# Retention's v projection first, on operands without norm and shift; new unit orders in both mixers; half of layer 0's mix through DRAM

## Chip and metric

One core of a Trainium2 chip runs the whole program in one launch. The metric is the device time of an execution in microseconds. A run without profile gives the time alone; one more execution was profiled, and all rows of the trace come from that one.

## What is computed

Two decoder layers over 1024 tokens of width 1024, all in float32. In each, a conditioning vector c gives by one large product six columns (shift, scale, gate for the mixer, the same for the MLP) of 1024 channels.

```
for layer in range(2):
    mod = silu(c) @ ada_w[layer] + ada_b[layer]              # 1024 x 6144
    sh_m, sc_m, gt_m, sh_f, sc_f, gt_f = split(mod, 6)
    h = rmsnorm(x, norm_mix_w[layer]) * (1 + sc_m) + sh_m
    y = even_mixer(h) if layer == 0 else odd_mixer(h)
    x = x + gt_m * y
    h = rmsnorm(x, norm_mlp_w[layer]) * (1 + sc_f) + sh_f
    x = x + gt_f * (square(relu(h @ w1)) @ w2)
return rmsnorm(x, final_norm_w)
```

The even mixer projects h to x, y (a gated linear recurrence, RG-LRU), and q, k, v, g (chunkwise retention with 4 heads of 128, rotary q and k, a norm per head, and a silu gate g). The odd mixer projects to Q, F, I, G (HGRN2) and q, k, v, z (gated DeltaNet). Both concatenate their two parts to `mix` and multiply by an output matrix.

## The kernel before

**Layout.** Activations lie with channels on partitions: x is 8 tiles of 128 channels for each of two halves (f) of 512 tokens. A projection is cut into units of 128 output channels: the 24 units of the even mixer are x0 to x3, y0 to y3 and q, k, v, g of the heads 0 to 3. For full precision every operand is split into a rounded high part (on ScalarE) and a low remainder (by a subtraction on VectorE), `split` (L599). `mm3` (L732) then does three matmuls for each of the 8 channel tiles, high x high, high x low and low x high, each 128x512: 24 dense matmuls for a unit and half, 48 for a unit.

**Order.** Every operation is recorded first (`Recorder`, L158), with an engine, a duration that is assumed, and a priority: its place in the program plus a bias. `place` (L218) then simulates the engines and lets each take, of what is ready and has free buffers, the operation with the lowest number. So the program order steers, and the order found is fixed for each engine. All DMAs go through SP's queue (a few through POOL's). Dense matmuls have the bias BIG, thus lowest priority: any other ready matmul goes ahead. Buffers: 73 tiles of 128x512 in `heap`, 4 of 128x1024 in `raw` (weights as loaded), 6 in `w` (their high and low parts, two for a unit), 3 PSUM banks `dps` for dense results and 5 `psum` for all others; `raw`, `w`, `dps`, `pad` and `blk` are given out in program order.

**Weights.** `push` (L623) loads the next unit into `raw` and splits it; `pop` (L684) keeps three ahead and, while the ninth to the fortieth unit are loaded, adds two ada units for each. An ada unit (`ada_unit`, L759) loads 512 KB of modulation rows into `raw` and multiplies them by csil (silu(c) on all partitions, a `blk` tile) with a running sum on VectorE: one of the 96 columns of `mod`. What is left of the 80 ada units is done in the down projection of layer 0's MLP, one in every third of its 112 steps from step 32 on (L1025). `ada_until(0)`, `ada_bias` and `ada_wsc` (L1440 to L1443) then finish the columns of layer 1, `wsc` being the scale times the norm's weight.

**Start (L1161 to L1218).** x half 0 is loaded, csil is made, and the norm factor of half 0 by squares, a sum over channels on TensorE and two activations (`rstd_half`, L797). Then for each of 8 channel tiles j: the shift column comes from 16 matmul passes with one output column (`ccol`) and a small transpose, the scale column from two multiplies with a running sum (512 wide, `blk`), and `first_operand` (L1180) makes h and splits it. Each j loads 1 MB of modulation rows. The first three weight units are split with the subtraction on POOL, and the norm of half 1 adds its squares on POOL too. Then `first = dense(hh, LEAD, pmt)` (L1407) does x0, x1 and q0 together.

**Mixer of layer 0 (L1406 to L1430).** The loop goes through EVEN_ORDER (L436); "l2" ends the recurrence of the two x units before it (`lru_out`, L1317). A v unit's result is copied out of PSUM, and `ret_item` (L1362) turns it by four transposes and an eviction (`to_token_major`, L1353) into tokens on partitions, which the two products with v need. `split_mix` (L1146) splits `mix` for `out_proj` (L847) and can fetch parts from the DRAM tensor `ms`; layer 0 keeps all of mix in SBUF, layer 1 sends that of its first three heads through `ms`. Layer 1's loop (L1823 to L1850) follows ODD_ORDER (L451) in the same way.

## Time and profile before

| | us |
|---|---|
| median of 3 runs | 2313.14 (2312.41 to 2313.26) |
| profiled execution | 2310.03 |
| its span, first to last instruction | 2308.3 |
| TensorE busy | 2272.8 |
| VectorE busy | 1698.1 |
| ScalarE busy | 1278.1 |
| units of layer 0's mixer, about | 24 to 350 |
| its output projection, about | 350 to 435 |
| MLP of layer 0, about | 435 to 1069 |
| mixer of layer 1 with its output projection, about | 1069 to 1650 |

Nearly all instructions are recorded by one helper, so every line reads L342; groups are told apart by the tiles that they write and read. Matmuls overlap, and their ends are modelled: the step from one start to the next is the pace, not the mean ns of one.

### The profile page before, as it was taken

To read this page: it belongs to the slowest core of one execution; us is meant where nothing else is said; L and a number is where in the kernel's file an instruction comes from. 1 tells how busy PE (TensorE), PEld (TensorE's weight loads), DVE (VectorE), ACT (ScalarE), POOL (GpSimd) and SP (SyncE) were. 2 spreads that over 40 slices of the span, in tenths; PEclk is the share of its full clock that TensorE was granted. 3 is DMA by queue.
4 is the path that set the end of the run, shared out by engine and by line. 5 is a ranking of instruction groups with operands and counts; after the bars stand their busy time and mean duration, and the time that the engine had idled before them with its cause. 6 is when DMAs were issued, how large, how long until landed. Compare 5 with 4: busy or idle time off the path is not lost.

```text
span 2308.3 us, 31439 instructions
## 1 busy us (share of the span) xinstructions
PE 2272.8 (98%) x10906; PEld 1868.4 (81%) x10906; DVE 1698.1 (74%) x2830; ACT 1278.1 (55%) x2377; POOL 330.7 (14%) x474
## 2 busy tenths in 40 slices
PE   7999999999999999999999999999999999999998
PEld 4778888878888888887887888878888888888886
DVE  7998668996665867888876687566687666765776
ACT  5788454575555444455755575646465555544444
POOL 3000000010000101000264335440001000111100
PEclk9999999999999999999999999999999999999999
DMA  8243338867665989643213122153358664997742
GB/s 296 82 135 121 113 119 287 285 188 230 193 183 159 335 299 307 213 147 99 77 44 81 50 61 69 57 153 125 127 170 253 193 192 146 292 301 231 178 133 96
DMA packets 199075, 393.34 MB, mean 170 GB/s; under 512 B 30146, under 2 KB 40962, under 8 KB 198916
## 3 DMA queue, kind: packets, MB, share of 16 engines
q1 hardware_dynamic: 180484, 357.78, 46.1%
q0 software_dynamic: 18432, 33.56, 9.0%
q8 instruction: 85, 1.39, 0.2%
q14 instruction: 74, 0.61, 0.1%
HBM read 308.91 MB, written 82.35 MB: 170 GB/s over the span
## 4 chain that ended last, share of the span: by engine, by line
PE 81%; issue 6%; DVE 5%; ACT 5%; DMA 3%; SPq 0%; POOL 0%; POOLq 0%; DVEq 0%; ACTq 0%
PE psum L342 41%; PE dps L342 40%; ACT heap L342 3%; DVE heap L342 3%; DMA raw<-in_dram 1%; DMA heap<-in_dram 1%; DVE w L342 1%; ACT w L342 1%; DMA heap<-h_spill 1%; DVE raw L342 1%; SPq L342 0%; DMA h_spill<-heap 0%; ACT L342 0%; ACT pad L342 0%; POOL heap L342 0%
## 5 line engine op out<-in xcount | busy, mean ns | idle before, releaser
L342 PE MATMUL dps<-heap,w 128*128 128x512 f32 x5016 | 1241.4, 395 | 7.7 <-DVE heap L342 4.1
L342 PEld LDWEIGHTS dps<-heap,w 128*128 128x128 f32 x5016 | 926.7, 188 | 200.9 <-DVE heap L342 6.4
L342 PE MATMUL psum<-heap,w 128*128 128x512 f32 x3816 | 890.5, 389 | 2.3 <-DVE heap L342 1.8
L342 PEld LDWEIGHTS psum<-heap,w 128*128 128x128 f32 x3816 | 715.7, 188 | 154.3 <-DVE heap L342 3.8
L342 ACT ACTIVATE heap<-heap 128x512 f32<-128x512 f32 (+2 forms) x1055 | 617.0, 609 | 184.3 <-DVE heap L342 162.2
L342 DVE TENSOR_TENSOR heap<-heap,heap 128x512 f32<-128x512 f32 (+1 forms) x863 | 579.7, 695 | 79.0 <-ACT heap L342 72.7
L342 ACT ACTIVATE w<-raw 128x512 fp32r<-128x512 f32 (+1 forms) x248 | 193.3, 782 | 219.5 <-PE dps L342 101.6
L342 ACT ACTIVATE w<-heap 128x512 fp32r<-128x512 f32 x224 | 141.5, 632 | 297.9 <-PE psum L342 274.8
L342 DVE TENSOR_TENSOR w<-raw,w 128x512 fp32r<-128x512 f32 (+1 forms) x213 | 194.3, 915 | 96.4 <-ACT w L342 90.7
L342 DVE TENSOR_TENSOR w<-heap,w 128x512 fp32r<-128x512 f32 x192 | 132.3, 689 | 120.0 <-ACT w L342 119.6
L342 POOL TENSOR_TENSOR blk<-blk,blk 32x31 f32<-32x31 f32 (+15 forms) x248 | 169.8, 685 | 34.2 <-issue 9.6
L342 POOL DMA_DIRECT2D raw<-in_dram x32 | 27.8, 870 | 768.9 <-DMA x_spill<-heap 283.2
L342 ACT ACTIVATE heap<-psum 128x512 f32<-128x512 f32 (+6 forms) x189 | 89.8, 482 | 82.8 <-PE psum L342 81.6
L342 PE MATMUL psum<-heap,heap 128*128 128x128 f32 (+4 forms) x1064 | 128.0, 264 | 2.2 <-DVE heap L342 1.7
L342 PEld LDWEIGHTS psum<-heap,heap 128*128 128x128 f32 (+2 forms) x1064 | 112.6, 169 | 21.6 <-DVE heap L342 3.9
L342 POOL DMA_DIRECT2D heap<-in_dram x64 | 55.7, 870 | 440.0 <-DMA heap<-in_dram 157.6
L342 DVE SCALAR_TENSOR_TENSOR raw<-raw,blk 128x1024 f32<-128x1024 f32 x80 | 97.0, 1218 | 4.7 <-DMA raw<-in_dram 4.7
L342 DVE TENSOR_TENSOR heap<-psum,heap 128x512 f32<-128x512 f32 x89 | 61.1, 687 | 41.6 <-PE psum L342 36.3
L342 ACT ACTIVATE heap<-dps 128x512 f32<-128x512 f32 (+1 forms) x134 | 77.7, 586 | 23.0 <-PE dps L342 14.1
L342 ACT ACTIVATE w<-pad 128x512 fp32r<-128x512 f32 x64 | 40.5, 633 | 88.6 <-PE psum L342 55.6
L342 DVE SCALAR_TENSOR_TENSOR heap<-pad,col,heap 128x512 f32<-128x512 f32 x96 | 78.3, 819 | 0.3
L342 DVE TENSOR_TENSOR w<-pad,w 128x512 fp32r<-128x512 f32 x64 | 44.1, 690 | 39.3 <-ACT w L342 39.2
(180 smaller groups left out, 1270.2 us busy)
## 6 DMA issues: line engine op xcount, KB each, us to landing
raw<-in_dram SPq DMA_DIRECT2D x232, 512.0 KB, 4.3
heap<-in_dram SPq DMA_DIRECT2D x226, 256.0 KB, 5.6
h_spill<-heap SPq DMA_DIRECT2D x224, 256.0 KB, 4.5
heap<-h_spill SPq DMA_DIRECT2D x224, 256.0 KB, 5.3
heap<-in_dram POOLq DMA_DIRECT2D x64, 256.0 KB, 6.7
x_spill<-heap SPq DMA_DIRECT2D x48, 256.0 KB, 2.9
heap<-x_spill SPq DMA_DIRECT2D x48, 256.0 KB, 5.3
pad<-in_dram SPq DMA_DIRECT2D x32, 256.0 KB, 2.8
```

The costliest lines, as they stand in the source:

```text
L342: op.call(*a, **k)
```

## The change

The four v units move to the front and no longer use h. For each j, as soon as its scale column and its x tile are there, `plain_operand` makes x times (1 + scale) times the norm's weight, split in two. `lead_tile` multiplies 128 tokens of it (as the stationary operand) by the 512 columns of all four heads' v weights, 24 dense matmuls for each of 8 token tiles, so that the result has tokens on partitions. The shift columns are computed afterwards, four of them on TensorE and four on VectorE. A ninth `lead_tile` on the shift columns, repeated over 128 tokens, gives `lead_bias`. The norm factor, turned to a column by eight transposes, multiplies the eight tiles, and lead_bias is added. `ret_item` reads these tiles. The squares of the norm wait for the last plain operand, and POOL takes no part. h is made after that, and units are then done one at a time. One ada unit goes with each of the loads 5 to 24, two with 25 to 40, and the rest with every third step of the down projection from step 28 on. Mix of heads 0 and 1 of both kinds goes through `ms`. Both orders of units are new.

```
 EVEN_ORDER = [(w[0], int(w[1])) for w in
-              "x0 x1 l2 q0 k0 v0 x2 x3 l2 q1 k1 v1 y0 y1 q2 k2 v2 y2 q3 k3 v3 y3 g0 g1 g2 g3".split()]
+              "x0 x1 q0 k0 x2 l2 q1 k1 x3 l2 q2 k2 y0 g0 q3 y1 k3 g1 g2 y2 y3 g3".split()]
 ODD_ORDER = [(w[0], int(w[1])) for w in
-             "q0 k0 v0 F0 Q0 I0 q1 k1 v1 G0 F1 Q1 q2 z0 I1 k2 v2 F2 G1 q3 Q2 k3 z1 z2 I2 F3 Q3 v3 G2 I3 G3 z3".split()]
+             "q0 k0 v0 F0 Q0 I0 q1 k1 v1 G0 F1 Q1 q2 k2 I1 z0 v2 F2 G1 q3 Q2 k3 I2 v3 z1 F3 Q3 z2 G2 I3 G3 z3".split()]
 def push():
-            split(hi, lo, raw, (), G if i < LEAD else V)
+            split(hi, lo, raw)
+    def lead_unit():
+        i = state["next"]
+        state["next"] = i + 1
+        raw = rec.tile("raw")
+        dma(raw, units[i])
+        if i < 3:
+            hi, lo = rec.tile("w", F32R), rec.tile("w", F32R)
+            split(hi, lo, raw)
+            lead_w.extend((hi[:, c], lo[:, c]) for c in (slice(0, HT), slice(HT, D)))
+        else:
+            for c in (slice(0, HT), slice(HT, D)):
+                hi, lo = hsplit_tiles()
+                split(hi, lo, raw[:, c])
+                lead_w.append((hi, lo))
 def pop():
-            if 8 < n <= 40:
-                ada_some(2)
+            if 4 < n <= 40:
+                ada_some(1 if n <= 24 else 2)
 def mlp(l, xh):
-            if l == 0 and n >= 32 and n % 3 == 1:
+            if l == 0 and n >= 28 and n % 3 == 1:
                 ada_some(1, [marks[-1]])
...
+    def plain_operand(f, j):
+        w = wsc[:, j:j + 1]
+        hi, lo = hsplit_tiles()
+        act(hi, xh[f][j], AF.Copy, scale=w)
+        plain[f].append((hi, lo))
+        return V.scalar_tensor_tensor(lo, xh[f][j], w, hi.bitcast(F32), ALU.mult, ALU.subtract)
     for j in range(KC):
+        if j % 2 == 0:
+            lead_unit()
+        xh[0].append(ht("x"))
+        dma(xh[0][j], xT[j, :, 0:HT])
+        for q in range(2):
+            a = ht("ada")
+            dma(a, ada[4 + j][:, q * HT:(q + 1) * HT])
+            V.scalar_tensor_tensor(a, a, 1.0, csil[:, q * HT:(q + 1) * HT], ALU.mult, ALU.mult,
+                                   accum_out=acc[:, j, q:q + 1])
...
+        plain_operand(0, j)
+    xh[1] = load_half(xT, 1)
+    for j in range(KC):
+        plain_done = plain_operand(1, j)
+    shift_raw = {}
+    for j in (0, 4, 1, 5, 2, 6, 3, 7):
+        for q in range(2):
+            a = shift_raw[j, q] = ht("ada")
+            dma(a, (ada0[j] if j < 4 else ada[j - 4])[:, q * HT:(q + 1) * HT])
+    rec.bias = 0
+    def lead_tile(ps, his, los):
+        mm3(ps, his, los, range(KC), [w[0] for w in lead_w], [w[1] for w in lead_w])
+        y = ht("y")
+        act(y, ps, AF.Copy)
+        return y
+    for f in range(2):
+        for n in range(4):
+            c = slice(n * P, n * P + P)
+            lead[f].append(lead_tile(pdt() if n < 3 else pmt(), [h[:, c] for h, _ in plain[f]], [l[:, c] for _, l in plain[f]]))
...
+    rs = [rstd_half(xh[f], after=[plain_done]) for f in range(2)]
...
+    lead_bias = lead_tile(pmt(), [a[0] for a in sh], [a[1] for a in sh])
+    pm, rstok = pmt(), small("rstok", [8])
+    for f in range(2):
+        for n in range(4):
+            T.transpose(pm[:, 4 * f + n:4 * f + n + 1], rs[f][0:1, n * P:n * P + P], ident[0:1, 0:1])
+    V.tensor_copy(rstok, pm[:, 0:8])
+    for f in range(2):
+        scaled(f, rs[f])
+        for k in range(KC):
+            hh[f].append(first_operand(f, k))
+    for f in range(2):
+        for n in range(4):
+            V.scalar_tensor_tensor(lead[f][n], lead[f][n], rstok[:, 4 * f + n:4 * f + n + 1], lead_bias, ALU.mult, ALU.add)
 def ret_item(h, f, q, k):
-        vt = to_token_major(vT)
+        vt = [v[:, h * P:h * P + P] for v in vtok[f]]
...
-    first = dense(hh, LEAD, pmt)
     for kind, h in EVEN_ORDER:
-        pss = first.pop(0) if first else dense(hh)
+        pss = dense(hh)
...
+            elif kind in "yg":
+                ch = h + (4 if kind == "g" else 0)
+                (lru_gelu if kind == "y" else gate_mix)(ps, mix[f][ch])
+                if h < 2:
+                    dma(ms[f, ch], mix[f][ch])
+                    mix[f][ch] = None
-    out_proj(split_mix(mix, late), xh, 0)
+    out_proj(split_mix(mix, late, ms), xh, 0)
```

## Rows read from the trace of the kernel before

**Rows 1.** The page, part 1: busy time of each engine, its share of the span, and instructions (x).

```profile
PE 2272.8 (98%) x10906; PEld 1868.4 (81%) x10906; DVE 1698.1 (74%) x2830; ACT 1278.1 (55%) x2377; POOL 330.7 (14%) x474
```

**Rows 2.** The windows view of stretches of the start and of the mixer of layer 0: length, then busy time and instructions (x) of TensorE's matmuls (PE), its weight loads (PEld), VectorE (DVE), ScalarE (ACT) and GpSimd (POOL), the granted clock (1.00 is 2.4 GHz), the DMA share and GB/s.

```profile
0.00:13.00 13.00, 3.89 (x17) 3.58 (x18) 7.13 (x25) 9.07 (x19) 1.34 (x7) 1.00 0.84 282
...
22.00:48.00 26.00, 22.88 (x135) 14.29 (x134) 23.22 (x48) 14.25 (x29) 14.67 (x8) 0.93 0.96 340
...
90.00:150.00 60.00, 58.92 (x295) 48.90 (x294) 58.70 (x114) 44.77 (x83) 1.01 (x1) 1.00 0.41 124
```

**Rows 3.** The windows view again, columns as in rows 2, of the rest of layer 0's mixer, of the mixer of layer 1, of 50 us within it, and of the end of layer 0's MLP.

```profile
90.00:350.00 260.00, 257.62 (x1297) 215.00 (x1296) 206.35 (x396) 173.54 (x393) 3.63 (x4) 1.00 0.40 121
1080.00:1660.00 580.00, 573.37 (x3259) 477.05 (x3259) 413.63 (x701) 348.61 (x696) 196.86 (x326) 0.99 0.27 82
1200.00:1250.00 50.00, 46.48 (x256) 39.18 (x255) 34.22 (x54) 32.09 (x62) 6.43 (x19) 0.93 0.32 87
1054.00:1069.00 15.00, 15.00 (x69) 12.08 (x68) 5.02 (x7) 4.51 (x7) 0.00 (x0) 1.00 0.27 90
```

**Rows 4.** Groups of TensorE's instructions from 0 to 90 us, shapes kept apart: what is written and read, shapes, count (x), busy us and mean ns of one, idle time before them and what ended it.

```profile
L342 PE MATMUL dps<-heap,w 128*128 128x512 f32 x120 | 31.0, 401 | 0.2 <-POOL w L342 0.2
...
L342 PE MATMUL psum<-heap,w 128*128 128x512 f32 x72 | 17.7, 396 | 0.8 <-DVE heap L342 0.6
...
L342 PE MATMUL psum<-heap,ones_f 1*128 1x512 f32 x4 | 2.2, 640 | 0.0
```

**Rows 5.** The timeline of TensorE in the start: start, length of the run of like instructions, what, count (x), idle time before it and what ended it.

```profile
12.86 3.15 PE L342 MATMUL psum<-heap,ccol 128*1 128x128 f32 x14 [3.13 <-DMA heap<-in_dram]
...
22.60 1.91 PE L342 MATMUL psum<-heap,ccol 128*1 128x128 f32 x16
...
32.20 3.53 PE L342 MATMUL psum<-heap,ccol 128*1 128x128 f32 x16 [2.23 <-DMA heap<-in_dram]
...
78.92 11.04 PE L342 MATMUL dps<-heap,w 128*128 128x512 f32 x48
89.80 0.39 PE L342 MATMUL psum<-heap,heap 128*128 128x512 f32 x1
```

**Rows 6.** The rates of all DMA queues from 0 to 60 us, GB/s in 40 slices of 1.5 us.

```profile
GB/s 0 145 305 269 320 361 403 374 410 403 392 382 389 404 388 391 377 389 385 382 384 386 388 388 382 392 392 364 184 57 186 336 388 264 6 11 0 0 0 0
```

**Rows 7.** The timeline of all engines from 9.5 to 19 us, columns as in rows 5.

```profile
9.77 0.60 ACT L342 ACTIVATE blk<-psum 128x512 f32<-128x512 f32 x1 [0.29 <-PE psum L342]
...
13.24 0.63 ACT L342 ACTIVATE heap<-heap 128x512 fp32r<-128x512 f32 x1
13.31 2.34 POOL L342 TENSOR_TENSOR w<-raw,w 128x1024 fp32r<-128x1024 f32 x1 [11.43 <-ACT w L342]
13.90 2.30 DVE L342 TENSOR_TENSOR heap<-heap,heap 128x512 fp32r<-128x512 f32 x1 [0.70 <-ACT heap L342]
...
16.12 0.68 DVE L342 SCALAR_TENSOR_TENSOR heap<-heap,blk 128x512 f32<-128x512 f32 x1
...
16.73 0.68 DVE L342 SCALAR_TENSOR_TENSOR heap<-heap,blk 128x512 f32<-128x512 f32 x1
...
18.23 0.16 DVE L342 SCALAR_TENSOR_TENSOR wsc<-mod,col 128x1 f32<-128x1 f32 x1
```

**Rows 8.** Groups of VectorE's instructions from 0 to 90 us, columns as in rows 4.

```profile
L342 DVE SCALAR_TENSOR_TENSOR heap<-heap,blk 128x512 f32<-128x512 f32 x16 | 16.1, 1011 | 0.0
L342 DVE TENSOR_TENSOR heap<-heap,heap 128x512 fp32r<-128x512 f32 x19 | 14.3, 772 | 4.8 <-ACT heap L342 4.6
...
L342 DVE TENSOR_TENSOR w<-raw,w 128x1024 fp32r<-128x1024 f32 x3 | 3.7, 1223 | 0.3 <-ACT w L342 0.3
L342 DVE SCALAR_TENSOR_TENSOR wsc<-mod,col 128x1 f32<-128x1 f32 x8 | 3.3, 415 | 0.0
```

**Rows 9.** The timeline of TensorE in the mixer of layer 1, columns as in rows 5.

```profile
1213.61 0.60 PE L342 MATMUL psum<-ident,heap 128*128 128x128 f32 x4
1213.96 0.48 PE L342 MATMUL psum<-heap,ones_r 128*128 128x512 f32 x1
1217.97 0.80 PE L342 MATMUL dps<-heap,w 128*128 128x512 f32 x1 [3.52 <-DVE heap L342]
```

**Rows 10.** The view of one tensor, the DRAM tensor that layer 1's mix already goes through: its transfers with the issue times in ns (min, median, max), first and last start, and the time from issue to landing in us.

```profile
L342 SPq DMA_DIRECT2D heap<-mix_spill x12: 320/423/639, 1545.0 to 1552.0; - x12
...
DMA to landing us min/median/max: 2.0/4.3/6.2
```

**Rows 11.** Groups of VectorE's instructions from 90 to 350 us, columns as in rows 4.

```profile
L342 DVE SCALAR_TENSOR_TENSOR raw<-raw,blk 128x1024 f32<-128x1024 f32 x37 | 45.0, 1217 | 3.5 <-DMA raw<-in_dram 3.5
...
L342 DVE SCALAR_TENSOR_TENSOR heap<-pad,col,heap 128x512 f32<-128x512 f32 x19 | 14.0, 743 | 0.0
```

**Rows 12.** The timeline of VectorE around the end of layer 0's MLP, columns as in rows 5.

```profile
982.61 1.22 DVE L342 SCALAR_TENSOR_TENSOR raw<-raw,blk 128x1024 f32<-128x1024 f32 x1
...
993.53 0.24 DVE L342 SCALAR_TENSOR_TENSOR wsc<-mod,col 128x8 f32<-128x8 f32 x2
...
1031.82 1.41 DVE L342 SCALAR_TENSOR_TENSOR heap<-heap,wsc,heap 128x512 f32<-128x512 f32 x2
...
1052.92 0.75 DVE L342 SCALAR_TENSOR_TENSOR heap<-heap,mod,heap 128x512 fp32r<-128x512 f32 x1
```

**Rows 13.** The timeline of TensorE there, columns as in rows 5.

```profile
1058.22 8.33 PE L342 MATMUL dps<-heap,w 128*128 128x512 f32 x36
```

More of the change, by code (lines that the diff above doesn't have):

```diff
@@ L606, in trunk_kernel @@
     units = []
+    lead_w = []
     loads = {}
@@ L760, in ada_unit @@
         a = rec.tile("raw")
-        dma(a, ada[48 * l + j - 8], after)
+        dma(a, ada[48 * l + j - 4], after)
         acc = mod[:, 48 * l + j:48 * l + j + 1]
@@ L794, in column_sum, with rstd_half @@
         T.matmul(ps, ones_x, lo, start=False, stop=True)
-    def rstd_half(xh, eng=V, last=False):
+    def rstd_half(xh, eng=V, last=False, after=()):
         order = (4, 5, 6, 7, 0, 1, 2, 3) if last else range(KC)
         ssum = ht("ssum")
-        act(ssum, xh[order[0]], AF.Square)
+        act(ssum, xh[order[0]], AF.Square, after)
         for k in order[1:]:
             sq = ht("sq")
-            act(sq, xh[k], AF.Square)
+            act(sq, xh[k], AF.Square, after)
             if not last or k != order[-1]:
@@ L1182, in first_operand @@
         act(h, xh[f][k], AF.Identity, scale=wsc[:, k:k + 1], bias=mod[:, k:k + 1])
-        hh[f].append(operand(h))
-    scaled(0, rs0)
+        return operand(h)
     acc = small("ada0", [8, 2])
-    hh = [[], []]
-    for j in range(KC):
-        if j in (0, 1, 3):
-            with bias(2 * BIG):
-                push()
+    plain = [[], []]
+    def plain_operand(f, j):
[4 more added lines that the diff above has]
+        return V.scalar_tensor_tensor(lo, xh[f][j], w, hi.bitcast(F32), ALU.mult, ALU.subtract)
@@ new lines, in trunk_kernel @@
+    for f in range(2):
+        for n in range(4):
+            c = slice(n * P, n * P + P)
+            lead[f].append(lead_tile(pdt() if n < 3 else pmt(), [h[:, c] for h, _ in plain[f]], [l[:, c] for _, l in plain[f]]))
+    for j in range(4, KC):
+        for q in range(2):
+            a = shift_raw[j, q]
+            V.scalar_tensor_tensor(a, a, 1.0, csil[:, q * HT:(q + 1) * HT], ALU.mult, ALU.mult,
+                                   accum_out=acc[:, j, q:q + 1])
+        V.scalar_tensor_tensor(mod[:, j:j + 1], acc[:, j, 0:1], cc("ada_b", j), acc[:, j, 1:2], ALU.add, ALU.add)
@@ L1192, in trunk_kernel @@
+    for j in range(4):
         pm, row = pmt(), rec.tile("s")
         for q in range(2):
-            a = ht("ada")
-            dma(a, ada0[j][:, q * HT:(q + 1) * HT])
+            a = shift_raw[j, q]
             for k in range(4):
@@ L1371, in ret_item @@
         pkv = pmt()
-        for s in sl4:
-            T.matmul(pkv[:, s], kt[:, s], vt[:, s], start=True, stop=True)
+        for n, s in enumerate(sl4):
+            T.matmul(pkv[:, s], kt[:, s], vt[n], start=True, stop=True)
         st = ht("st")
@@ L1383, in ret_item @@
         po = pmt()
-        for s in sl4:
-            T.matmul(po[:, s], sc[:, s], vt[:, s], start=True, stop=before is None)
+        for n, s in enumerate(sl4):
+            T.matmul(po[:, s], sc[:, s], vt[n], start=True, stop=before is None)
             if before is not None:
@@ L1821, in hg_item @@
         act(m, pot, AF.Copy, scale=cc("hnw"))
-    first, got, fg = dense(hh, LEAD), {}, {}
+    first, got, fg = dense(hh, 3), {}, {}
     for kind, h in ODD_ORDER:
```

54 lines of the change are left out of this document (22 added, 32 removed).

## The prediction

> **What bounds it now.** I read the page first: TensorE is busy 98% of the span, VectorE 74% [rows 1]. So time can come from two places only: TensorE work that disappears, and stretches in which TensorE waits or runs slowly. The windows view places the second kind [rows 2]: in the first 13 us TensorE works 3.9, and between 22 and 48 us it works 22.9 of 26 with the granted clock at 0.93 on the mean. After 90 us it loses little: in 260 us to the end of layer 0's mixer it idles 2.4, and 6.6 of 580 us in the mixer of layer 1 [rows 3]. The loss is in the start.
>
> How large is it? The instruction groups of the first 90 us [rows 4] count 120 + 72 = 192 dense 128x512 matmuls, four units of the 24 of layer 0. Warm, 48 of them took from 78.92 to 89.80 us [rows 5], 0.2267 us each, so 192 are worth 43.5 us. They were done at 89.8 us. The other 46 us hold the modulation columns, the norm, and waiting. The timeline [rows 5] shows why: x0, x1 and q0 need the shift, the scale and the norm of all 1024 channels, thus 8 MB of modulation rows, and the DMA engines deliver 380 to 400 GB/s without a gap from 10 to 41 us [rows 6].
>
> **What the change does there.** The four v units come first, on x times its scale column only. The norm factor multiplies the result per token, and the shift comes back as one added row, lead_bias. The sum is made for the moment at which TensorE has done 192 dense matmuls and all preparation, 89.8 us now.
>
> 1. First dense matmul. csil is complete at 9.77 + 0.60 = 10.4 us [rows 7]. Constants, one v unit, one tile of x and one scale row are 1.5 MB, there by 7.5 us by the rates of [rows 6]. After csil: the second accumulating multiply at its pitch of 0.61, two one-column operations of 0.16 and the rounded half on ScalarE, 0.63 [rows 7], with hand-overs: 12.5 us.
> 2. Feeding it. A step of eight needs one x tile, one scale row and half a v unit, 1.05 MB, 2.7 us at 390 GB/s. VectorE pays 2 x 0.61 + 0.4 + 0.65 for the low half, and half of a weight split of 1.22 [rows 8]: 2.9 us. TensorE consumes a step in 12 matmuls, 2.72 us. All three are nearly equal, and TensorE starts on the slow clock, so I charge no wait: the eighth operand is wanted at about 35 us; VectorE has it at 10.4 + 8 x 2.9 = 33.6 and DMA at 26.
> 3. Dense work, 192 x 0.2267: 43.5 us.
> 4. The slow clock. The one-column passes took 3.15 us for 14 from 12.86 and 1.91 for 16 from 22.60 [rows 5]: the clock column has nothing on it, but by this pace TensorE went from 1.2 to 2.4 GHz only at about 22 us, after working from 12.86 on with small gaps. That is 9.5 us at half rate. The fall after an idle 2.23 us near 30 us lasted 3.6 us (0.93 over 26) [rows 2], a later one, amid dense matmuls, 7 us (0.93 over 50) [rows 3]. A dense start is nearest to the last: 7 us at half rate, 3.5 us lost; the bounds are 0 and 4.8. The Trainium skill (TensorE: Matmul & The Clock Gate, "What's actually happening") has the slow state as the default, which activity releases; by it every start pays something here, and the lower bound would fall away.
> 5. Modulation on TensorE: shift columns 0 to 3 stay, 64 passes, 4 x 1.91 plus four small transposes, 8.2 us. Shift columns 4 to 7 go to VectorE. All shift rows now travel on SP's queue behind the second half of x, 6.3 MB more, so they are complete near 42 us; lead_bias, the first to want them, comes at 59.
> 6. As before, four column sums 512 wide, 0.9, and the position passes, 2.2 [rows 4]: 3.1 us.
> 7. New: lead_bias, 24 x 0.2267 = 5.4, and eight one-row transposes, 0.7 by the pitch in [rows 9]: 6.1 us.
> 8. New wait between the v units and x0. The six w tiles hold three v units until lead_bias has read them, and the next split behind it is 1.06 on ScalarE plus 1.22 on VectorE; lead_bias frees them one unit at a time, so I take 2 us, bounds 0 and 10. The upper end is h itself being late. VectorE after 33.6: second-half operands 8 x 0.65, shift multiplies 4 x 1.42, 14 norm adds x 0.65, four low halves 2.6, then 1.3 for each h operand: half 0 is ready near 66 us and half 1 near 77. TensorE has other work until 12.5 + 43.5 + 3.5 + 8.2 + 3.1 + 6.1 = 76.9. Half 0 has a lead of 10 us, which is the cover.
>
> Sum: 76.9 + 2 = 78.9 against 89.8, a gain of 10.9 us.
>
> **The rest of the change.**
> 9. Each retention item loses four transposes of v: 32 at 0.35 us per four [rows 9], 2.8 us of TensorE work gone. Eight copies and eight evictions on ScalarE go as well, hidden before.
> 10. mix for heads 0 and 1 through DRAM: eight writes and eight reads of 256 KB, all on SP's queue, among raw and h loads. A read of this kind landed in at most 6.2 us [rows 10], and it may start two units (22 us) ahead of the output projection, where DMA has a share of 0.40 [rows 3]. Nothing on the path. If the cover went, 4 to 6 us.
> 11. VectorE's bill before x3: 16 low halves of plain x (10.4), four shift columns more (5.7), eight rescalings (5.5), three weight splits and seven norm adds that POOL did (3.7 + 4.6), 1.3 for the shift: 31 us more. Less: 12 ada units fewer while the units of layer 0 run (one with each of 20 loads in place of two with each of 16), 12 x 1.22 = 14.6 [rows 11], and the slow VectorE operations at POOL's side, next point.
> 12. POOL leaves the start. A VectorE subtraction beginning at 13.90, beside POOL's 2.34 us, took 2.30 us; the multiplies behind it, alone, took 0.68 [rows 7]. All 16 of these averaged 1011 ns in the first 90 us, the low halves 772, the wsc columns 415 [rows 8]; over 0.68, 0.68 and 0.16 that is 5.3 + 1.7 + 2.0 = 9 us in excess. So I take the lone pitch in step 2. At 1011 ns a step would cost VectorE 3.7 us, eight of them 6.4 us more, and the gain of the start would be 4.5 in place of 10.9. The Trainium skill (SBUF — State Buffer, "Who interferes with whom") gives a cause: a VectorE instruction with two SBUF inputs and a GpSimd instruction that reads SBUF exclude each other; by that rule it is 10.9, and the trace agrees for the pair at 13.31 and 13.90.
> 13. The 12 ada units reappear in the down projection of layer 0, whose last such unit now ends at 983 us, with the scale columns at 993 and the layer-1 norm of half 0 from 1031 to 1053 [rows 12]. They are three steps (8.2 us) apart, so the last one comes just before the tail of 48 matmuls whose first 36 begin at 1058 [rows 13]. The norm of half 0, 16 x 0.7 = 11 us of VectorE, then runs from about 1062, beside that tail; between 1054 and 1069 VectorE is busy for 5.0 of 15 us [rows 3]. TensorE wants its first operand at 1069 and takes 2 us for each, VectorE gives one in 1.4. I charge 1 us, bounds 0 and 6. Behind it on VectorE are the sums of half 1.
> 14. Layer 1's order changes from its fourteenth unit on. The longest wait, 3.5 us at 1218 [rows 9], and the slow clock beside it [rows 3] lie in the unit after v1 and G0, ahead of that; they stay. Of the later 3.1 us I credit nothing; bounds: 3.1 gained or as much lost. The same for the 2.4 us of layer 0.
>
> Total: 10.9 + 2.8 - 1 = 12.7 us. The profiled execution took 2310.0 (span 2308.3, 1.7 around it), the median of the runs 2313.1, 3.1 more; I subtract from the median: **2300 us**.
>
> **Rivals.**
> - **VectorE becomes the bound until about 150 us.** It is busy 58.7 of 60 us between 90 and 150 [rows 2], so it has no room for 31 - 9 = 22 us more. It decides if VectorE is still behind when the first retention item needs its rope. Then TensorE waits 22 us there, and the time is 2300 + 22 = 2322, slower than before. Against: at equal TensorE progress the change has done four v units, nearly free for VectorE, in place of x2 and x3, whose taps alone cost it 2 x 3 x 0.74 = 4.4 us each [rows 11], and 14.6 us of ada units are put off. Chance 0.12.
> - **h is late and the clock falls again.** Step 8 at its upper end, 8 us more, and another 7 us at half rate, 3.5: nearly all is given back, 2312. For it: a fall did follow 2.2 us of idling [rows 5]. Against: the 10 us of cover. Chance 0.08.
> - **The boundary at 1069 us costs its 5 us**: 2305. Chance 0.15.
> - **More is gained**: fast clock from the first dense matmul (3.5), no wait in step 8 (2), the later waits of both mixers gone (5.5): 2289. Chance 0.15.
> - The forecast, 2295 to 2305: 0.50.
>
> **How the numbers follow.** About 0.2% (4.6 us) is what a measurement of this kernel can tell from no change. Faster takes the forecast, the boundary case and the larger gain: 0.80; the same, the late h: 0.08; slower, VectorE: 0.12. The range runs from just below the larger gain, 2288, to 2311, which leaves out the slower case and a part of the late one.
>
> **What would show it.** Dense matmuls from 12 to 13 us and 192 of them done by about 60; the first gate matmul of x0 no later than 80; no POOL work between 2 and 60 us; VectorE's blk multiplies near 680 ns; 64 passes with ccol instead of 128; wsc of layer 1 at about 1062 instead of 993, with TensorE busy across 1069 minus the gain. It is wrong if TensorE waits for VectorE more than 5 us between 60 and 160 us, if the v matmuls wait for DMA, or if waits in layer 1 sum to more than 10 us.

## The result and the profile after

The changed kernel takes **2294.47 us** (median, 2293.91 to 2295.03) against 2313.20 for the kernel before in the same session (2312.41 to 2314.78): a ratio of 0.9918, 95% interval 0.9901 to 0.9935, or 18.7 us less. The profiled execution took 2293.91 (span 2292.1); the two profiled spans differ by 16.2 us, because the profiled execution of the kernel before lay 3.1 under its median. The decomposition below explains the 16.2.

Part 1 of the page: busy time of each engine, share, instructions. It answers to [rows 1].

```profile
PE 2259.0 (99%) x10838; PEld 1862.1 (81%) x10838; DVE 1710.2 (75%) x2884; ACT 1287.3 (56%) x2385; POOL 312.1 (14%) x464
```

The windows view of the changed kernel (columns as in [rows 2]): the start; the first LRU units; the rest of layer 0's mixer; layer 1's mixer; 50 us around its first long wait; the boundary of the layers. They answer to [rows 2, 3].

```profile
0.00:13.00 13.00, 3.75 (x16) 3.48 (x16) 6.88 (x31) 5.95 (x13) 1.33 (x7) 1.00 0.82 278
13.00:20.00 7.00, 6.33 (x21) 5.10 (x22) 6.92 (x17) 3.62 (x6) 0.00 (x0) 1.00 1.05 410
20.00:76.00 56.00, 56.00 (x278) 43.09 (x277) 51.75 (x113) 43.64 (x76) 0.00 (x0) 1.00 0.64 227
90.00:150.00 60.00, 60.00 (x284) 49.32 (x283) 58.38 (x124) 34.82 (x56) 0.00 (x0) 1.00 0.31 96
90.00:350.00 260.00, 255.49 (x1272) 212.84 (x1271) 217.46 (x429) 182.76 (x404) 3.66 (x4) 1.00 0.36 110
1067.00:1645.00 578.00, 573.33 (x3263) 475.63 (x3262) 412.76 (x706) 351.47 (x698) 197.90 (x326) 1.00 0.27 82
1186.00:1236.00 50.00, 48.20 (x268) 39.83 (x266) 35.05 (x56) 32.24 (x59) 7.81 (x21) 1.00 0.33 100
1043.00:1058.00 15.00, 15.00 (x67) 11.52 (x67) 14.93 (x24) 9.43 (x13) 0.00 (x0) 1.00 0.75 205
```

From 20 to 76 us TensorE is busy for 56.00 of 56. POOL has no work there. VectorE is busy for 58.38 of 60 us between 90 and 150, as full as before, and TensorE loses nothing by it (60.00 of 60). Layer 0's mixer idles 4.5 us in 260, more than before (2.4); layer 1's idles 4.7 in 578 and its granted clock is 1.00, where before it idled 6.6 in 580 at 0.99; 1.4 of the 4.7 are the wait at the boundary.

TensorE's timeline, answering to [rows 5, 9]: the first dense matmul, x0's first, the positions that follow, the boundary's wait, and the place in layer 1 where 3.52 us were waited before.

```profile
13.68 2.93 PE L342 MATMUL dps<-w,heap 128*128 128x512 f32 x6 [4.82 <-ACT heap L342]
...
75.83 10.43 PE L342 MATMUL dps<-heap,w 128*128 128x512 f32 x44
86.42 8.26 PE L342 MATMUL dps<-heap,w 128*128 128x512 f32 x35 [0.17 <-DVE heap L342]
94.62 1.98 PE L342 MATMUL psum<-heap,ones_f 1*128 1x512 f32 x4
...
1073.19 0.40 PE L342 MATMUL psum<-heap,wgs 128*16 128x512 f32 x1 [1.38 <-ACT heap L342]
...
1199.66 0.60 PE L342 MATMUL psum<-ident,heap 128*128 128x128 f32 x4
1200.01 1.64 PE L342 MATMUL dps<-heap,w 128*128 128x512 f32 x6
1201.49 1.05 PE L342 MATMUL psum<-heap,heap 128*128 128x128 f32 x8
1202.30 0.70 PE L342 MATMUL psum<-heap,ones_r 128*128 128x512 f32 x2
1202.84 1.05 PE L342 MATMUL psum<-heap 128*128 128x128 f32 x8
1203.73 0.60 PE L342 MATMUL psum<-ident,heap 128*128 128x128 f32 x4
1205.74 2.13 PE L342 MATMUL dps<-heap,w 128*128 128x512 f32 x8 [1.41 <-DVE heap L342]
```

What the kernel before did behind its 3.52 us at 1217.97 (TensorE's timeline of the kernel before, continuing [rows 9]):

```profile
1218.56 1.06 PE L342 MATMUL psum<-ident,heap 128*128 128x128 f32 x4
...
1221.12 1.91 PE L342 MATMUL psum<-heap,heap 128*128 128x128 f32 x8
1222.83 1.40 PE L342 MATMUL psum<-heap 128*128 128x128 f32 x8
1224.06 0.60 PE L342 MATMUL psum<-ident,heap 128*128 128x128 f32 x4
```

VectorE's groups of the first 90 us, answering to [rows 8], and its timeline at the boundary, answering to [rows 12]: the last multiply of an ada unit, and the scale columns of layer 1.

```profile
L342 DVE SCALAR_TENSOR_TENSOR heap<-heap,blk 128x512 f32<-128x512 f32 x24 | 15.7, 686 | 0.7 <-ACT blk L342 0.7
...
L342 DVE TENSOR_TENSOR w<-raw,w 128x1024 fp32r<-128x1024 f32 x7 | 8.6, 1222 | 1.9 <-ACT w L342 1.9
```

```profile
1038.16 1.23 DVE L342 SCALAR_TENSOR_TENSOR raw<-raw,blk 128x1024 f32<-128x1024 f32 x1 [0.64 <-DMA raw<-in_dram]
...
1043.48 0.25 DVE L342 SCALAR_TENSOR_TENSOR wsc<-mod,col 128x8 f32<-128x8 f32 x2
```

**Where the time came from.** Both kernels do the same dense matmuls from x0 on, so the traces can be laid side by side by the number of gate, projection and MLP matmuls still to come. The table gives how far each kernel is ahead of the kernel before at such a point (us; worked out from the start times of these matmuls in the profiled executions). The other columns belong to the experiments below.

| matmuls left (time before) | after | e1 old odd order | e7 start alone | e4 old ada plan | e10 POOL executes | e9 POOL planned |
|---|---|---|---|---|---|---|
| 8039 (271 us) | 13.7 | 14.0 | 4.9 | -4.5 | 8.6 | -14.6 |
| 4799 (1021) | 14.1 | 14.2 | 5.3 | -4.5 | 8.4 | -14.1 |
| 4199 (1191) | 12.1 | 12.2 | 5.4 | -4.4 | 6.4 | -17.0 |
| 4079 (1231) | 18.8 | 18.8 | 5.4 | -3.4 | 13.0 | -10.4 |
| 2639 (1694) | 17.1 | 4.2 | 5.6 | -18.6 | 11.4 | -12.0 |
| 119 (2268) | 15.8 | 4.3 | 5.7 | -19.8 | 9.4 | -12.2 |

So the start and layer 0's mixer gave 13.7 us, the boundary took 2.0, layer 1's mixer behind 1191 us gave 4.9 (17.1 - 12.1), and its MLP took 1.3, in which TensorE waits 1.51 us at 2020 us that it did not wait before.

The row of 1231 us is no price of the wait near 1218 alone. There the two kernels have different small matmuls behind them: one dense matmul earlier the lead is 17.9, one later 17.1. Taken by parts, between 1191 and 1694 us TensorE idles 3.2 us where it idled 6.6, which is 2.1 less at the wait near 1218 and 1.3 less at the later ones. It works none of the time at half clock where before 5.6 us ran so, worth 2.8. The matmuls themselves take 1.2 us more. Together, 2.1 + 1.3 + 2.8 - 1.2, these make the 4.9 but for rounding.

### The profile page after: what moved, and what is told of

The parts are those of the page before. It is cut to its first block, busy times and chain, and to the rows that moved or that the text cites. A ratio compares the mean times of both kernels' runs of the same rounds, so it can differ in the third digit from the quotient of the medians.

```text
span 2292.1 us, 31384 instructions
## 1 busy us (share of the span) xinstructions
PE 2259.0 (99%) x10838; PEld 1862.1 (81%) x10838; DVE 1710.2 (75%) x2884; ACT 1287.3 (56%) x2385; POOL 312.1 (14%) x464
## 4 chain that ended last, share of the span: by engine, by line
PE 85%; issue 6%; ACT 4%; DVE 3%; DMA 2%; SPq 0%; POOL 0%; POOLq 0%; DVEq 0%; ACTq 0%
PE dps L342 44%; PE psum L342 41%; ACT heap L342 3%; DVE heap L342 2%; DMA heap<-in_dram 1%; ACT w L342 1%; DVE w L342 0%; DMA heap<-h_spill 0%; DMA raw<-in_dram 0%; ACT L342 0%; DVE raw L342 0%; SPq L342 0%; POOL heap L342 0%; ACT pad L342 0%; DVE blk L342 0%
## 5 line engine op out<-in xcount | busy, mean ns | idle before, releaser
L342 PE MATMUL dps<-heap,w 128*128 128x512 f32 x4896 | 1213.2, 395 | 5.4 <-DVE heap L342 3.3
L342 PEld LDWEIGHTS dps<-heap,w 128*128 128x128 f32 x4896 | 903.9, 188 | 190.0 <-DVE heap L342 5.4
L342 PE MATMUL psum<-heap,w 128*128 128x512 f32 x3744 | 873.3, 389 | 1.5 <-DVE heap L342 1.2
L342 PEld LDWEIGHTS psum<-heap,w 128*128 128x128 f32 x3744 | 702.3, 188 | 149.6 <-DVE heap L342 2.7
L342 POOL TENSOR_TENSOR blk<-blk,blk 32x31 f32<-32x31 f32 (+15 forms) x248 | 171.3, 691 | 32.1 <-DMA blk<-n_full 14.6
L342 ACT ACTIVATE heap<-psum 128x512 f32<-128x512 f32 (+5 forms) x182 | 85.4, 475 | 55.9 <-PE psum L342 55.5
L342 DVE SCALAR_TENSOR_TENSOR raw<-raw,blk 128x1024 f32<-128x1024 f32 x80 | 97.0, 1218 | 0.6 <-DMA raw<-in_dram 0.6
L342 POOL DMA_DIRECT2D pad<-in_dram x32 | 28.3, 912 | 353.4 <-ACT heap L342 196.5
```

Source lines behind the costliest of these rows:

```text
L342: op.call(*a, **k)
```

## The experiments

The kernel before ran beside each: 2311.5 us (median) with e1 to e4, 2313.2 with e5 to e8, 2313.0 with e9 to e11, 2312.1 with e12.

### Layer 1: the order of units, or the ada plan?

**e1** takes back the order of layer 1 alone, **e2** makes it alone, **e4** takes back the plan of the ada units.

```
e1, on the changed kernel:
-ODD_ORDER ... "... q2 k2 I1 z0 v2 F2 G1 q3 Q2 k3 I2 v3 z1 F3 Q3 z2 G2 I3 G3 z3"
+ODD_ORDER ... "... q2 z0 I1 k2 v2 F2 G1 q3 Q2 k3 z1 z2 I2 F3 Q3 v3 G2 I3 G3 z3"
e2, on the kernel before: the reverse
e4, on the changed kernel:
-            if 4 < n <= 40:
-                ada_some(1 if n <= 24 else 2)
+            if 8 < n <= 40:
+                ada_some(2)
...
-            if l == 0 and n >= 28 and n % 3 == 1:
+            if l == 0 and n >= 32 and n % 3 == 1:
```

> The change with layer 1's old order of units, all else new. Theory A (the new order took away the 3.5 us wait behind G0 and with it the fall of the clock): the wait is back near 1205 us, the clock falls beside it, and the time is 2298 to 2301 us. Theory B (the wait lies ahead of the first unit that moved, so the order has nothing to do with it; it went because the end of layer 0's MLP now shifts VectorE's work): the time is 2293 to 2296 us, with no wait above 2 us between 1180 and 1240 us and no fall of the clock.

> The kernel before with layer 1's new order of units and nothing else. Theory A: the wait of 3.5 us at 1218 us and the fall of the clock beside it go, 2306 to 2310 us. Theory B: both stay, 2311 to 2315 us; only the later waits (3.1 us in all) may change.

> The change with the old plan of ada units: two with each of the loads 9 to 40, the other 16 from step 32 of the down projection on. Theory A (VectorE has room for 12 more units of 1.22 us between 76 and 350 us, since its waits there come from chains and not from load): the waits between 90 and 350 us stay near 4.5 us, the wait of 1.4 us at 1073 us goes, and the time is 2292 to 2295 us. Theory B (VectorE is at its limit until about 150 us, and the lighter ada plan is what makes the gain possible): waits between 90 and 350 us rise by 5 to 15 us, and the time is 2299 to 2309 us.

e1 took 2305.81 us, ratio 0.9972 (0.9961 to 0.9983). Up to 1243 us of its trace it is the changed kernel, the small wait near 1204 included: what was gained there is not the order's doing, as in theory B. Behind that it falls 13 us back (table, 4.2 against 17.1), so the time is out of both theories' ranges. TensorE's timeline of e1:

```profile
1470.45 1.82 PE L342 MATMUL dps<-heap,w 128*128 128x512 f32 x4 [0.98 <-DVE heap L342]
...
1481.42 0.49 PE L342 MATMUL psum<-s,heap 128*128 128x128 f32 x2 [1.78 <-ACT s L342]
...
1485.30 0.79 PE L342 MATMUL dps<-heap,w 128*128 128x512 f32 x1 [1.83 <-DVE heap L342]
```

Between 1479 and 1485 us a chain of small matmuls stands there with no dense one put between them (in these 60 us TensorE starts 101 dense matmuls; in the changed kernel's it starts 182), and the clock falls twice (windows view of e1, columns as above):

```profile
1440.00:1500.00 60.00, 52.85 (x333) 45.01 (x332) 31.52 (x60) 32.95 (x81) 31.25 (x59) 0.91 0.10 29
```

e2 took 2331.48, ratio 1.0086 (1.0071 to 1.0100): slower than the kernel before, which neither theory had. The wait near 1218 stays, as in theory B (3.52 us of idling, 3.78 from start to start of the matmuls; waits without a fence below are given from start to start, some 0.15 more than the idling that a view shows), and others follow at 1357 to 1363, 1496 to 1505 and 1516 to 1536 us, with four falls of the clock. e4 took 2329.05, ratio 1.0069 (1.0057 to 1.0081). The boundary's wait at 1073 is gone, as expected of the moved units, but its layer 1 shows e2's waits again at the same places, and layer 0 lost 18 us against the changed kernel, mostly in one wait. TensorE's timeline of e4:

```profile
263.61 1.22 PE L342 MATMUL psum<-heap,heap 128*128 128x128 f32 x4 [16.38 <-DVE heap L342]
```

Between 90 and 350 us it idles 18.5 us in place of 4.5, a rise that theory B had (5 to 15); the clock then falls behind the wait, layer 1 loses as well, and the time is far over B's range. VectorE is not fuller there than in the changed kernel (213.6 us busy against 217.5), which speaks against its load as the cause.

What follows: the wait near 1218 shrinks with the new ada plan, whatever the order (1.41 us in e1 and in the changed kernel; 3.52 in e2, e4 and e7). The order's own worth depends on that plan: with the new plan the new order is worth 13 us (e1), with the old plan it costs 14 to 17 (e4 and e2 between the points at 1191 and 1694 us). Neither of the two edits has a price of its own.

### The start alone, and layer 0's order

```
e7, on the changed kernel: e4's edit; both orders as before (v left out of layer 0's); and
-                if h < 2:
-                    dma(ms[f, ch], mix[f][ch])
-                    mix[f][ch] = None
...
-    out_proj(split_mix(mix, late, ms), xh, 0)
+    out_proj(split_mix(mix, late), xh, 0)
e5, on the changed kernel:
-              "x0 x1 q0 k0 x2 l2 q1 k1 x3 l2 q2 k2 y0 g0 q3 y1 k3 g1 g2 y2 y3 g3".split()]
+              "x0 x1 l2 q0 k0 x2 x3 l2 q1 k1 y0 y1 q2 k2 y2 q3 k3 y3 g0 g1 g2 g3".split()]
```

> The kernel before with the new start alone: v units first with tokens on partitions and corrected at eviction; old ada plan, old orders in both layers (v left out of layer 0's), mix in SBUF. Theory A (the parts add up): the start's 12.0 us and the 1.8 us of the rest of layer 0 are gained against the kernel before and nothing else: 2311.5 - 13.8 = 2297.7 (2295 to 2301); the wait of 3.8 us near 1218 - 14 = 1204 us with 6.8 us at half clock stays. Theory B (the new start moves work that VectorE did early into the time of layer 0's first LRU units, and only the other orders and the ada plan make room): at least one wait of 8 us or more in 150 to 270 us, and a time of 2305 or more.

> The changed kernel with the order of units in layer 0's mixer put back to the old one (without its v units): both LRU blocks earlier, all y before all g. Start, moved ada units, mix through DRAM and layer 1's order stay. Theory A (the parts add up; a unit's place costs only what TensorE executes): within 3 us of the changed kernel, 2291 to 2298, layer 1's waits as there. Theory B (the order written by hand and the loads of VectorE and ScalarE fit only together): the second LRU block, 18 us on ScalarE, meets TensorE at another point: a wait of 8 us or more with a stretch at half clock between 180 and 260 us, and a time over 2302. Layer 1's own waits (1.6 us near 1204 us and none near 1218) are to stay by both, since its order and the ada plan are untouched.

e7 took 2306.40, ratio 0.9972 (0.9961 to 0.9983). x0's first dense matmul came at 76.56, so the start itself was had; one wait in layer 0 took most of it back, and layer 1's wait stayed as it was. TensorE's timeline of e7:

```profile
226.93 3.35 PE L342 MATMUL dps<-heap,w 128*128 128x512 f32 x7 [10.06 <-ACT heap L342]
...
1212.50 0.80 PE L342 MATMUL dps<-heap,w 128*128 128x512 f32 x1 [3.52 <-DVE heap L342]
```

The clock was at half from 221.6 to 231.8 us, so the first 4.9 us of work behind the wait ran at half rate. Theory B holds. e5, with the new ada plan and the old order of layer 0, took 2294.58, ratio 0.9922 (0.9908 to 0.9935): no difference from the changed kernel that the runs can tell. Its waits (1.7, 1.5, 1.7 us near 166, 222 and 229) sum to what the changed kernel has at 189, 192 and 244 (0.9, 2.0, 2.0). Theory A holds: layer 0's new order is worth nothing measurable once the ada units are moved. e4 differs from the changed kernel by the plan alone, and waited 16.4 us near 247. In layer 0 it is the plan of the ada units that lets the start's gain through.

### POOL in the start: its work, or the order made for it?

The planner lays down every engine's order from assumed durations. **e3** gives 3 weight subtractions and 7 additions of half 1's norm to POOL. **e9** lets it plan them so and has VectorE execute them; **e10** plans them on VectorE and has POOL execute them.

```
e3, on the changed kernel:
-            split(hi, lo, raw)
+            split(hi, lo, raw, (), G)
...
-    rs = [rstd_half(xh[f], after=[plain_done]) for f in range(2)]
+    rs = [rstd_half(xh[f], V if f == 0 else G, after=[plain_done]) for f in range(2)]
e9: G above becomes an object with Pool's costs in the plan that issues on nc.vector
e10: G above becomes an object with Vector's costs in the plan that issues on nc.gpsimd
```

> The change with three weight subtractions of the v units and the seven norm adds of half 1 on POOL again. Theory A (POOL and VectorE exclude each other in two-input work, and VectorE is what feeds TensorE in the start): the multiplies with csil average above 850 ns in place of 686, the first x0 matmul comes 4 to 8 us after the 75.8 us of the change, and the time is 2298 to 2302 us. Theory B (VectorE has slack there): the multiplies slow down but the first x0 matmul comes within 1.5 us of 75.8, and the time is 2293 to 2296 us.

> The planner is told that POOL does the 3 subtractions of the weights and the 7 additions of half 1's norm (so every engine has the order of e3_pool_back), but VectorE executes these 10. With e3_pool_back, with the changed kernel and with the next run this makes a table of two orders by two engines. Theory A (POOL's work on the chip is what costs: VectorE's operations beside it are longer and half 1 comes late): the waits of 9.6 us near 205 and of 16.7 us near 252 us go, time 2294 to 2298. Theory B (the order that the planner made is what costs, whoever executes): VectorE's multiplies are at 0.69 us again but both waits stay within a third of their lengths, time 2314 or more.

> The other corner: every engine's order is that of the changed kernel, as planned with these 10 operations on VectorE, but POOL executes them (3 subtractions of 2.4 us and 7 additions of 1.8 us). Theory A (POOL's work costs): multiplies at 0.97 us, the start some 1 to 3 us later, waits of 5 us or more after 150 us, time 2305 or more. Theory B (the order costs): the start 1 to 4.5 us later, the same waits as in the changed kernel near 189, 192 and 244 us, each under 3 us, time 2295 to 2300.

| | VectorE executes | POOL executes |
|---|---|---|
| planned on VectorE | changed kernel: 2294.47 | e10: 2300.17, ratio 0.9942 (0.9930 to 0.9954) |
| planned on POOL | e9: 2320.79, ratio 1.0035 (1.0021 to 1.0049) | e3: 2323.31, ratio 1.0046 (1.0034 to 1.0058) |

By these medians POOL's work costs 2.5 to 5.7 us, the order 23 to 26; the ratios' intervals overlap in each row, so only the order's share is clear of noise. In e3 the multiplies are at 971 ns, x0's first dense matmul comes at 76.91, only 1.1 us later than in the changed kernel, as in its theory B; the loss, which neither theory had, is made behind it by two waits, 9.6 us near 205 and 16.7 near 252. In e9 POOL does nothing between 2 and 60 us and VectorE's multiplies are back at 686 ns, yet both waits stand as in e3, to within 0.02 us. The first is ended by VectorE, which finishes the scans of an LRU block behind ScalarE's part of it. The timelines of ScalarE and of TensorE in e9 show the second:

```profile
244.73 6.50 ACT L342 ACTIVATE heap<-heap 128x512 f32<-128x512 f32 x12 [2.54 <-DVE heap L342]
251.24 1.28 ACT L342 ACT_TABLE_LOAD   x1
...
264.44 1.65 ACT L342 ACTIVATE heap<-heap 128x512 f32<-128x512 f32 x3
...
266.19 0.57 ACT L342 ACTIVATE heap<-dps 128x512 f32<-128x512 f32 x1
```

```profile
247.09 3.21 PE L342 MATMUL dps<-heap,w 128*128 128x512 f32 x13
266.81 4.63 PE L342 MATMUL dps<-heap,w 128*128 128x512 f32 x10 [16.51 <-ACT heap L342]
```

ScalarE runs the second LRU block (its part of the recurrence of two x units) in its fixed order, with two table loads, and the eviction of a dense result, its copy out of PSUM (heap<-dps), stands behind all of it, at 266.19; TensorE's next dense matmul needs that buffer. ScalarE's timeline in the changed kernel has the block's table load at 222.28, and evictions of dense results before it and within it:

```profile
220.41 1.19 ACT L342 ACTIVATE heap<-dps 64x512 f32<-64x512 f32 x2
...
222.28 1.28 ACT L342 ACT_TABLE_LOAD   x1
...
235.84 1.06 ACT L342 ACTIVATE heap<-dps 128x512 f32<-128x512 f32 x2
```

An eviction within the block is not enough by itself: in e4 one stands there too (at 243.39), and TensorE's wait lasts until VectorE is nearly through the block's scans, between which stand two evictions of its own.

Theory B of e9 holds for the waits and the time. e10 shows what POOL's work does by itself: VectorE's multiplies rise to 822 ns (in e3, with the other order, 971) and the norm comes late. VectorE's group in e10 and TensorE's timeline there:

```profile
L342 DVE SCALAR_TENSOR_TENSOR heap<-heap,blk 128x512 f32<-128x512 f32 x24 | 19.0, 822 | 1.5 <-ACT blk L342 1.5
```

```profile
53.55 0.50 PE L342 MATMUL psum<-heap,ones_r 128*128 128x512 f32 x1 [1.98 <-ACT heap L342]
...
56.26 0.50 PE L342 MATMUL psum<-heap,ones_r 128*128 128x512 f32 x1 [1.08 <-DVE heap L342]
...
80.89 10.45 PE L342 MATMUL dps<-heap,w 128*128 128x512 f32 x44
```

The means hide how it happens. In e10 three of the 24 multiplies take 1.75 to 1.89 us and the others 0.68; in e3 five take 1.44 to 2.89. These eight are the ones that start while POOL is in a two-operand operation, and each ends 0.54 to 0.56 us behind POOL's end. Two of them in e3's timeline of all engines, each under POOL's line:

```profile
12.92 2.37 POOL L342 TENSOR_TENSOR w<-raw,w 128x1024 fp32r<-128x1024 f32 x1 [2.89 <-ACT w L342]
13.41 2.42 DVE L342 SCALAR_TENSOR_TENSOR heap<-heap,blk 128x512 f32<-128x512 f32 x1 [0.99 <-DMA heap<-in_dram]
...
18.39 2.40 POOL L342 TENSOR_TENSOR w<-raw,w 128x1024 fp32r<-128x1024 f32 x1 [3.11 <-ACT w L342]
18.45 2.89 DVE L342 SCALAR_TENSOR_TENSOR heap<-heap,blk 128x512 f32<-128x512 f32 x1
```

In e10, x0 starts 5.1 us later than in the changed kernel: 3.8 us are waits of TensorE, and 0.6 a slow clock that lasted longer at the start (its dense matmuls start 0.43 us apart until about 18 us, the changed kernel's until about 17). The waits behind it are the changed kernel's own (0.9, 2.0, 2.0). Theory B had 1 to 4.5 us for the start, and a time up to 2300; both were just passed.

### Two terms of the sum

```
e8, on the changed kernel, in ret_item (results unused):
+        transposes(q)
e6, on the changed kernel: the mix of heads 0 and 1 stays in SBUF (the last two hunks of e7)
```

> The changed kernel with four more transposes of q, that nobody reads, ahead of each of the 8 retention items: 32 more on TensorE in all, as many as the change took out by bringing v with tokens on partitions. Theory A (a term of the sum: 32 times the start-to-start time of a transpose, 0.09 us): 2.8 us slower than the changed kernel, 2296 to 2299. Rival (by the rows' own busy time, 0.18 us each): 5.9 us slower, 2299 to 2302. Theory B (static orders): over 2304 with a new wait of 5 us or more in layer 0's mixer, so that the price of the transposes themselves can't be read.

> The changed kernel with the mixes of heads 0 and 1 of layer 0 kept in SBUF: 8 writes to DRAM and 8 loads less. Theory A (the prediction's step 10: both lie behind other work, and what they free is SBUF): 0 to 2 us from the changed kernel, if the planner finds room for 8 tiles of 2 KB a partition more; no wait near the start of the output projection (350 to 360 us). Theory B (without the room, raw weight tiles and operands of the units behind come later): waits of 2 us or more between 250 and 350 us on a tile's release, time over 2299.

e8 took 2301.01, ratio 0.9949 (0.9936 to 0.9961). At 7319 matmuls left it is 6.8 us behind the changed kernel, though x0 began 0.5 us earlier: 7.3 us in layer 0. The windows view of e8 gives 6.1 us of idling against 4.5, so 1.6 us are waits, and a fall of the clock (3.4 us at half) another 1.7:

```profile
90.00:350.00 260.00, 253.89 (x1271) 210.84 (x1270) 210.99 (x418) 176.93 (x395) 3.66 (x4) 0.99 0.34 106
```

The 32 transposes are left with 7.3 - 1.6 - 1.7 = 4.0 us, 0.125 each: between theory A's 2.8 and the rival's 5.9. But eight of them lie between 8039 and 7319 matmuls left, where neither kernel has a wait that counts or a slow clock, and these cost 0.69 us, 0.086 each, which is theory A's pitch. Whether the other 24 cost more by themselves, or by the other order planned around them, isn't shown.

e6 took 2298.11, ratio 0.9935 (0.9923 to 0.9948), some 3.6 us slower than the changed kernel, by neither theory: up to 380 us it loses nothing, without a wait of B's kind. It then falls 1.1 us behind up to 480, by waits of 0.2 to 0.3, 1.0 more up to 830 (a wait of 0.9 at 793), 0.4 at the boundary and 0.5 after 2000, in all 3.0 of the 3.7 us between the profiled executions. The transfers through DRAM cost nothing that shows, and the kernel without them is slower (the two ratios' intervals just overlap, the times do not). Whether by room in SBUF or by the other order planned for it, these runs don't tell.

### A faster version?

```
e11, on the changed kernel, in lead_unit:
-            split(hi, lo, raw)
+            split(hi, lo, raw, first_act[:1] if i == 1 else ())
... (first_act holds the roundings of plain_operand)
e12: e11 and e5 together
```

> The changed kernel with ScalarE's half of the second weight unit's split made to wait for the first operand's rounding (in the trace of the changed kernel the split went first, 1.06 us, and the first dense matmul came at 13.68). Theory A (the first operand sets the start): first dense matmul at 12.5 to 12.7, x0's first at 74.7 to 74.9, the time 1.0 us less than the changed kernel. Theory B (TensorE then meets a late operand or the gate of the clock, and the orders behind it shift): a first wait of 0.5 us or more before 50 us, and a gain under 0.4 us or a loss.

> Two edits that each were worth nothing on their own clock of the whole, together: the second weight unit's split behind the first operand (e11_start: x0's first dense matmul 0.9 us earlier, given back by one fall of the clock at 245 us) and layer 0's old order (e5_old_even: 4.8 us of waits as in the changed kernel, at other places and with no fall of the clock behind them, but 1.3 us lost at the start at half clock). Theory A (terms add up): no fall of the clock in layer 0, 1 us less than the changed kernel, 2292.5 to 2294. Theory B (each new plan has its own waits): waits of layer 0's mixer differ from e5_old_even's by 2 us or more, and the time is 2294 or more.

e11 took 2294.40, ratio 0.9920 (0.9907 to 0.9934). TensorE's timeline of e11:

```profile
12.48 6.31 PE L342 MATMUL dps<-w,heap 128*128 128x512 f32 x18 [3.60 <-ACT heap L342]
...
74.96 10.43 PE L342 MATMUL dps<-heap,w 128*128 128x512 f32 x44
```

At the start 0.9 us were gained, as by theory A, and given back by one fall of the clock (3.4 us at half) behind the wait at 243 us, which the changed kernel has too, without the fall. e12 took 2293.39 (2292.04 to 2294.47), ratio 0.9919 (0.9906 to 0.9933). Its waits in layer 0 are e5's, with no fall there, so theory A. The 1.1 us by which it beats the changed kernel are less than the intervals can tell.

## Why the prediction was right, and where it was not

The forecast was 2300, faster; measured were 2294.5, 5.5 less: inside the range, and just below the 2295 to 2305 of the forecast case. The mechanism of the start was right: x0 starts as early as summed, within 1.1 us, and with the new start alone (e7) as well. The terms of the start and of layer 0's mixer came out at 13.7 us together, as summed (10.9 + 2.8), but by errors that cancel, which is luck. The sum of 12.7 gives 2300.4; the 5.9 from there are 2.5 by which the two medians differ more than the two profiled executions, and 4.9 in layer 1's mixer (step 14), plus 0.4 in layer 0's MLP and 0.4 behind the last MLP matmuls, less 1.0 at the boundary and 1.3 in layer 1's MLP.

- **Step 1** (12.5 us): 13.68. ScalarE took the second unit's weight split (1.06 us) ahead of the first operand's rounding; with that put right the first dense matmul came at 12.48 (e11). The step had left out what else stood in ScalarE's queue.
- **Steps 2, 3:** right. No wait of TensorE between 20 and 76 us. The 192nd dense matmul began at 70 us and not by 60, since the shift passes and column sums ran among them and not behind; that changes no sum.
- **Step 4** (3.5 us lost to the slow clock): about 1.7, again with nothing on it in the clock column. The 24 dense matmuls from 13.68 to 20.86 took 7.2 us where 24 x 0.2267 is 5.4: the first eight started 0.43 us apart or more, those behind 17.2 us 0.23. In e5 the same 24 took 7.6 us, with the clock column at half until 18.9, so the amount varies. By the Trainium skill (TensorE: Matmul & The Clock Gate, "What's actually happening"), which has the slow state as the default, every start pays something, and these two did. The fall that the step took as its nearest case (0.93 over 50) began within the wait of 3.52 us, and not amid dense matmuls.
- **Steps 5 to 7:** the small passes took longer among dense ones. Between 35.2 and 75.8 us stand 129 dense matmuls, 29.2 us, so the rest, charged at 8.2 + 0.9 + 0.7 = 9.8, took 11.4.
- **Step 8** (wait of 2): 0.17. Half 0's cover held. Altogether the equal point, x0's start with the positions still to do, is 75.83 + 2.0 = 77.8 against 78.9: a gain of 12.0 for a predicted 10.9.
- **Step 9** (2.8 us): 1.7 net. That is what 13.7 - 12.0 leaves behind the start, and 2.1 us more idling in [rows 3]'s stretch are in it, so the work that went is worth about 3.8. e8 leaves 4.0 for 32 transposes by subtraction, but 0.086 for one where nothing disturbs, which is the pitch in [rows 9]. So the pitch may be right, and what the other 24 cost stays open. The added waits are within the bounds that step 14 gave layer 0.
- **Step 10** (nothing): right for the path; the gain by leaving SBUF (e6, 3.6) was not foreseen. The view of the spill tensor, answering to [rows 10], shows transfers, the reads among them, that landed in at most 6.7 us:

```profile
L342 SPq DMA_DIRECT2D heap<-mix_spill x20: 319/382/512, 325.7 to 1537.6; - x20
...
DMA to landing us min/median/max: 2.0/4.7/6.7
```

- **Step 11** and the rival that VectorE becomes the bound: VectorE was full until 150 us and TensorE did not wait for it there. The rival fell, by the reason given against it. Losses of that size exist all the same, with another mechanism: at 271 us e4, e7 and e9 are 18, 9 and 28 us behind the changed kernel (table), by waits for an LRU block in the fixed orders of ScalarE (e7, e9's second) and of VectorE behind it (e4, e9's first).
- **Step 12:** right. Multiplies at 686 ns for 1011, and 5.1 us of the start if POOL executes the ten (e10), where the step had 6.4. In one and the same order of VectorE the multiply takes 686 or 822 ns on the mean, and each multiply that started beside POOL's work ended just behind it (e3, e10). The rule of the Trainium skill (SBUF — State Buffer, "Who interferes with whom") that the step names agrees.
- **Step 13** (1 us, bounds 0 to 6): the place was right, and 2.0 us were lost at the boundary, 1.38 of them at 1073.19. VectorE was busy for 14.93 of the 15 us before 1058, fuller than the step had it; e4 and e7, with the old plan, lose nothing there. The scale columns came at 1043, which is 1058 on the clock of the kernel before, where the step had 1062.
- **Step 14** is the step that failed: "they stay". The wait at 1218 shrank from 3.52 to 1.41 us and the slow clock beside it went, 2.1 + 2.8 = 4.9 us. Comparing orders by hand, I took a wait ahead of the first moved unit for one that could not change. In both kernels 4104 dense matmuls are left when this wait ends. But by the new ada plan 20 small matmuls (1201.49 to 1203.73) are placed ahead of it, some 2.05 us of work, which is the 2.1 that the wait lost; before, TensorE waited first and did such ones behind it (1218.56 to 1224.06). Of the later waits nothing was credited; they fell from 3.1 to 1.8 us, and the matmuls' own time rose by nearly as much.

The rival "more is gained" (2289) came in part: 1.8 of the 3.5 for the clock at the start, 1.8 of the 2 of step 8, 1.3 of layer 1's later waits, while layer 0's waits grew by 2.1. The 4.9 us near 1218, the larger part of what the forecast lacked, it did not name.

## What to carry to other kernels

Where a planner fixes each engine's order in advance, cost an edit twice: by the work it moves, and by the order that is planned anew behind it; no wait behind the edit can be taken to stay. Ask of each block that an engine runs in one piece of its fixed order (here 18 to 22 us of ScalarE) what stands behind it in that queue and which buffer waits for that. To tell a slow operation from a bad order, plan with one duration and execute with the other, both ways. And when two traces are compared at a count of matmuls, read the lead at several counts: where the small matmuls lie differently, one reading can be off by the size of the effect.

## What the runs showed of the hardware

- A long wait is paid again behind its end. The granted clock fell within the waits of 9.5 and 16.5 us (e3), 10.1 (e7) and 16.4 (e4; idling, as in the views), and TensorE's next 4.4, 5.2, 4.9 and 6.7 us of work ran at half, which adds 2.2 to 3.3 us to each wait. These are the times from the wait's end to the clock's return in the records (219.4, 274.0, 231.8 and 270.3 us).
- A short wait is followed by a fall or not: the wait of 1.9 us that ends near 245 had none in the changed kernel and 3.4 us at half in e11, where the wait is the same to within 0.01 us. This alone moves a time by 1.7 us.
- A VectorE multiply of two operands that starts while POOL is in a two-operand operation ends 0.54 to 0.56 us behind POOL's end, in all eight such cases of e3 and e10; the others take 0.68 us. Where the multiply came first (e10, 18.45 us), it took 0.68, and POOL's operation from 18.70 on took 2.68 us in place of 2.35 to 2.37. So the multiplies' share of POOL's price goes by how many of them meet it, and for how long: three of 24 multiplies in e10 (822 ns on the mean), five in e3 (971), none without POOL (686).
- The clock column missed the slow clock of the changed kernel's start: the dense matmuls from 13.68 to 16.8 us started 0.43 us apart or more, where the column says 1.00. In e5 pace and column agree (0.43 apart, half until 18.9).
